# Four token mixers on one core: the order of all engines written out from an estimate, and weights split piece by piece

## The chip, the core and the metric

The kernel runs on one core of a Trainium2 chip. The metric is the device time of one execution in microseconds (us). A core has five instruction streams that run side by side and wait for each other through semaphores: PE (matrix products), DVE and ACT (element work on 128 partitions), POOL (a slower engine for element work) and SP (here it only issues DMAs). Each stream is executed in the order in which the program holds it, so a stream whose next instruction waits also holds up all that stands behind it.

## The reference, cut to what matters

Two layers, 256 tokens of width 1024, all in float32. The change concerns the middle step of each layer.

```python
x += 0.5 * rms(swiglu(rms(x)))             # FFN 1, inner width 2816
h = rms(x); p = h @ W_in                   # one projection, cut into column groups
y_nsa  = nsa_mixer(q, k..., v..., gates)   # 4 heads: compressed + selected + window
y_ret  = retention_mixer(q, k, v, g_in)    # 4 heads, chunks of 128
y_rwkv = rwkv7_mixer(p[rwkv columns])      # 4 heads, recurrence over chunks of 64
y_swa  = banded_attention(q, k, v, 128, sinks)
merged = sum(sigmoid(gate_m(h)) * (y_m @ P_m) for m in the four mixers)
x += rms(merged @ W_out)
x += 0.5 * rms(swiglu(rms(x)))             # FFN 2
```

Every weight matrix is read once per layer from HBM. Products with weights are made in three passes over numbers cut into a high and a low part (high x high, high x low, low x high), so each weight tile is first loaded raw, then copied to its high part by ACT (`whi`) and subtracted to its low part by DVE (`wlo`). This pair of instructions is called a split below.

## The kernel before, in words

The program runs FFN 1, the mixers, the product with W_out (`rows_out`) and FFN 2, twice. The change touches the mixers alone; instructions of the FFN stages and of `rows_out` are the same in both programs.

In the mixers there are two kinds of PE work. *Bulk* work has weights: projections into 512, 332 or 320 columns (`bulk_proj`, bank name `pj`), the four RWKV projections of 256 columns (`rwkv_proj`, `rwp`) and the branch products (`branch_block`, `z`). Each chunk `c` of the contraction takes three matmuls for each of the two token tiles `t` (`mm3`, L174 to L176). *Light* work has none: transposes (`tr`), attention scores (`sc`), the 32x32 solves of RWKV (`px`, `pq`), its recurrence (`pz`, `pu`, `psn`). Light work comes in chains: a few matmuls, then DVE, ACT or POOL instructions on their result, then the next matmuls.

`weave` writes the two kinds out in one list. Each light chain is a generator (a strand) that yields a number, the nanoseconds after which its next step may stand, or the name of a result that it needs. `weave` keeps one clock, `self.clk`, that only matmuls move, with a fixed cost for each. When a strand's time has come it is run, and otherwise the next piece of bulk work. Bulk pieces come in the order of the list `bulk`, the first whose inputs are done. After 2500 ns of light work in a row bulk is forced (`LIGHT`). What `weave` makes is only a priority: a list scheduler then places the instructions of each engine, with its own idea of when each could start, and splits of weights are lifted ahead by `high_priority(PRI)` in `stream`. Each bulk item calls `stream` for all its weights when it starts.

Memory: raw weights rotate through 4 buffers and split weights through 6 (`wraw`, `wsplit`), bulk results through 3 PSUM banks (`psA`), light results through 5 (`psB`), other mixer tiles through 29 buffers of 2 KB and 19 of 1 KB a partition (`NS2`, `NK1`).

Names used below. `pss` (L556) are the sums of squares of the RWKV keys: they need `sq` on DVE (L1061), and through POOL's `krs` and DVE's `rsb` they lead to `prs` and `kn` (L1084, L1087), then `bh` (L1092) and `ln`. `nsark` is the rotated key of the sparse attention, made by POOL (L545) and transposed by PE. `acc` (L1345) is the first use of a branch product `z`. `sm` (L602) is the softmax that is transposed next.

Of the kernel before, what the change touches and what calls it, by code (L numbers as in the profile page):

```python
# [21 lines left out]
NT = 2  # L22
# [78 lines left out]
NS2, NK1 = 29, 19  # L101
TAIL = 3
FL = 4
CY = 420
PRI, PRI2 = 60, 150
HOLD = 3
PROJ = (3, 1, 0, 2, 4, 5)
BRANCHES = (0, 1, 2)
WARM = 12
LIGHT, LIGHT_LOW = 2500.0, 425.0  # L110


class Trunk:
    def __init__(self, tc, A, out, layers=L, dbg=None):
        self.tc, self.nc, self.A, self.out = tc, tc.nc, A, out
        self.layers = layers
        self.dbg = dbg or {}
        self.uid = 0
        self.clk = self.light = 0.0
        self.pending = []  # L120
        self.feat = 0
# [46 lines left out]
    def mm3(self, out, a, b, first, last):  # L168

        mm = self.nc.tensor.matmul  # L170
        d = 3 * max(109.0, 2.5 + b[0].shape[-1] / 2.4)
        self.clk += d
        self.light = max(0.0, self.light - d)
# [14 lines left out]
    def psA(self, name="pa"):  # L188
        return self.ps.tile([P, 512], F32, tag="A", bufs=3, name=self.nm(name))

    def psB(self, name="pb"):
        return self.ps.tile([P, 512], F32, tag="B", bufs=5, name=self.nm(name))
# [39 lines left out]
    def pre_norm(self, t, xT, ss=None):  # L232
# [17 lines left out]
        def half(b):  # L250
# [6 lines left out]
            nc.vector.tensor_tensor(lo[:, 4 * b:4 * b + 4, t * P:(t + 1) * P], pv, dh.bitcast(F32), op=ALU.subtract)  # L257

# [188 lines left out]
    def bulk_proj(self, l, xT, c0, n, evac, key, lat=900, skew=False):  # L447

        w = [self.stream(self.A["w_in"][l][h * 512:(h + 1) * 512, c0:c0 + n], 4, n) for h in range(2)]
        pp = [self.psA("pj") for _ in range(NT)]  # L450
        order = [(c, t) for t in range(NT) for c in range(KC)] if skew else \
            [(c, t) for c in range(KC) for t in range(NT)]
        for c, t in order:
            if skew and t and c == 0:
                self.flush()
            ts_ = slice(t * P, (t + 1) * P)
            self.mm3(pp[t][:, 0:n], (xT[0][:, c, ts_], xT[1][:, c, ts_]), w[c // 4](c % 4, slice(0, n)),
                     c == 0, c == KC - 1)
            if t or skew:
                yield  # L460
        for t in range(NT):
            evac(t, pp[t])
        self.fin(key, lat)
# [4 lines left out]
    def fin(self, key, lat):  # L468
        self.done[key] = self.clk + lat

    def weave(self, strands, bulk):


        live = [[0.0, None, g] for g in strands]
        self.live = live
        cur, force = None, False
        while live or bulk or cur:
            ran = False

            if self.light > LIGHT:  # L480
                force = True
            elif self.light <= LIGHT_LOW:
                force = False
            if force and cur is None:
                cur = self.next_bulk(bulk)
            for s in [] if force and cur is not None else list(live):
# [4 lines left out]
                if s[0] > self.clk:  # L491
                    continue
                try:
                    r = next(s[2])
                    if isinstance(r, str):
                        s[1] = r
                    else:
                        s[0] = self.clk + r
                except StopIteration:
                    live.remove(s)  # L500
                ran = True
                break
            if ran:
                continue
            if cur is None:
                cur = self.next_bulk(bulk)
            if cur is not None:
                try:
                    next(cur)
                except StopIteration:  # L510
                    cur = None
                continue
            nxt = [s[0] for s in live if s[1] is None] + [self.done[s[1]] for s in live if s[1] in self.done]
            nxt += [self.when(b[0]) for b in bulk]
            nxt = [x for x in nxt if self.clk < x < 1e18]
            assert nxt, ([s[1] for s in live], [b[0] for b in bulk])
            self.clk = min(nxt)

    def next_bulk(self, bulk):
        for b in bulk:  # L520
            if self.when(b[0]) <= self.clk:
                bulk.remove(b)
                return b[1]

    def spawn(self, g):
        self.live.append([self.clk, None, g])
# [20 lines left out]
    def transposes(self, srcs):  # L547

        pt = self.psB("tr")
        for j, s in enumerate(srcs):  # L550
            self.nc.tensor.transpose(pt[:, j * P:(j + 1) * P], s, self.ident)  # L551
            self.tick(109)
        return pt

    def mm(self, out, a, b, cost, start=True, stop=True):
        self.nc.tensor.matmul(out, a, b, start=start, stop=stop)  # L556
        self.tick(cost)

    def mm4(self, out, a, b):

        for g in range(4):
            gs = slice(32 * g, 32 * g + 32)
            self.mm(out[gs], a[:, gs], b, 34)

    def tick(self, cost):
        self.clk += cost
        self.light += cost


    def attention(self, t, groups, score, pv, sink, mask_off, gate, evac):  # L570
# [6 lines left out]
        for e in range(groups):  # L577
# [10 lines left out]
            nc.vector.tensor_scalar(nm, mx, -SCALE, None, op0=ALU.mult)  # L588
            for i in range(2):
                nc.scalar.activation(sm[:, i, :], sm[:, i, :], AF.Exp, bias=nm[:, i:i + 1], scale=SCALE,  # L590
                                     accum_out=den[:, i:i + 1])
            if sink is not None:
                es = self.small(2, "es")
                nc.vector.tensor_add(es, nm, sink[1](e))
                nc.scalar.activation(es, es, AF.Exp)
                nc.vector.tensor_add(den, den, es)
# [8 lines left out]
        yield 6600  # L605
# [7 lines left out]
        yield 2400  # L613
        po = self.psB("po")
        for j in range(2):
            terms = list(zip(*[pv(j, hh, pts) for hh in range(2)]))
            for k, pair in enumerate(terms):
                for hh, (v, pT) in enumerate(pair):
                    self.mm(po[64 * hh:64 * hh + 64, j * P:(j + 1) * P], v, pT, 135, k == 0, k == len(terms) - 1)
# [13 lines left out]
    def swa(self, l, xT):  # L633
# [6 lines left out]
        def evac(t, ps):  # L640
            nc.scalar.activation(pv[t], ps[:, 0:512], AF.Copy)
            self.spawn(after(t))

        def after(t):
# [6 lines left out]
            yield 8820  # L651
# [3 lines left out]
            self.fin(f"swa_qk{t}", 749)  # L655
# [857 lines left out]
```

## Time and profile before

| | us |
|---|---|
| median of three runs (lowest, highest) | 1392.92 (1392.23, 1393.69) |
| profiled execution, its own time | 1393.8 |
| its span, first to last instruction | 1392.0 |
| mixers of the first layer, first bulk matmul to the first of W_out | 200.6 to 483.8 |
| mixers of the second layer | 887.5 to 1172.6 |

PE is busy for 1348.1 us of the span, 97%; DVE for 65%, ACT for 50%, POOL for 15%. The DMA engines are busy for about half to two thirds of the time. A matmul's busy time reaches into the next one's, since PE overlaps them; what a matmul costs in a row of equal ones is the step from start to start.

### The profile page before, as it was taken

The numbers are of one execution on the slowest core, as the hardware profiler recorded it, in microseconds if no ns is written. First come the engines' busy times: TensorE is split into PE (matmuls) and PEld (weight loads), VectorE is DVE, ScalarE is ACT, GpSimd is POOL, SyncE is SP. The second block draws the span as 40 slices with busy tenths as digits, with TensorE's granted clock in tenths as the row PEclk, the third lists the DMA queues.
The fourth block names the chain that finished last, engine by engine and source line by source line (L and its number), as shares of the span: only waits on it lengthen the run. The fifth ranks groups of instructions, "written<-read, shape, count | busy, mean of one in ns | idle before, by whom it ended". The sixth has DMA issues, their size and how long they took to land.

```text
span 1392.0 us, 24466 instructions
## 1 busy us (share of the span) xinstructions
PE 1348.1 (97%) x9756; PEld 1139.1 (82%) x9756; DVE 903.9 (65%) x1417; ACT 699.1 (50%) x1110; POOL 205.5 (15%) x269
## 2 busy tenths in 40 slices
PE   8999999898999999999999999998999999999998
PEld 7888878776778889888898888787777888888886
DVE  6666467748766666665566664687487656766643
ACT  6555456425344455564555554554353445555542
POOL 1000022603332110000000000335035220100000
PEclk9999999999999999999999999999999999999999
DMA  8865553435346646755647656434453556476662
GB/s 269 282 186 189 184 181 112 153 115 188 104 155 195 182 152 202 220 184 182 212 152 240 186 180 220 147 117 137 144 177 93 161 188 195 139 224 183 184 192 77
DMA packets 166146, 243.02 MB, mean 175 GB/s; under 512 B 9216, under 2 KB 120320, under 8 KB 165904
## 3 DMA queue, kind: packets, MB, share of 16 engines
q1 hardware_dynamic: 165248, 239.31, 54.3%
q8 instruction: 76, 1.25, 0.4%
q0 software_dynamic: 352, 1.10, 0.3%
q10 hardware_dynamic: 432, 1.05, 0.2%
q14 instruction: 38, 0.31, 0.1%
HBM read 240.38 MB, written 1.05 MB: 173 GB/s over the span
## 4 chain that ended last, share of the span: by engine, by line
PE 79%; DVE 8%; POOL 5%; ACT 3%; issue 2%; DMA 2%; POOLq 0%; DVEq 0%; SPq 0%; ACTq 0%
PE pf L209 20%; PE pf L210 10%; PE dn L174 6%; PE dn L176 6%; PE dn L175 6%; PE pj L174 6%; PE pj L176 5%; PE pj L175 5%; PE tr L551 1%; PE pg L175 1%; PE pg L174 1%; PE pg L176 1%; PE z L174 1%; DVE wlo L148 1%; PE z L176 1%
## 5 line engine op out<-in xcount | busy, mean ns | idle before, releaser
L148 DVE TENSOR_TENSOR wlo<-raw,whi 128x1024 fp32r<-128x1024 f32 (+1 forms) x420 | 516.7, 1237 | 295.1 <-ACT whi L147 292.2
L147 ACT ACTIVATE whi<-raw 128x1024 fp32r<-128x1024 f32 (+1 forms) x420 | 436.7, 1047 | 363.9 <-PE pj L176 90.4
L209 PE MATMUL pf<-xs,whi 128*128 128x512 f32 x1184 | 419.0, 399 | 0.0
L210 PE MATMUL pf<-xs,wlo 128*128 128x256 f32 x1184 | 332.5, 281 | 0.0
L209 PEld LDWEIGHTS pf<-xs,whi 128*128 128x128 f32 x1184 | 222.4, 188 | 54.9
L210 PEld LDWEIGHTS pf<-xs,wlo 128*128 128x128 f32 x1184 | 223.7, 189 | 0.0
L174 PE MATMUL pj<-whi,xs 128*128 128x512 f32 (+2 forms) x448 | 178.9, 399 | 1.0 <-DVE retg L912 1.0
L176 PE MATMUL pj<-whi,xs 128*128 128x512 f32 (+2 forms) x448 | 172.6, 385 | 0.0
L175 PE MATMUL pj<-wlo,xs 128*128 128x512 f32 (+2 forms) x448 | 172.0, 384 | 0.0
L174 PE MATMUL dn<-whi,hhi 128*128 128x512 f32 x352 | 137.3, 390 | 0.0
L175 PE MATMUL dn<-wlo,hhi 128*128 128x512 f32 x352 | 137.2, 390 | 0.0
L176 PE MATMUL dn<-whi,hlo 128*128 128x512 f32 x352 | 137.0, 389 | 0.0
L218 POOL TENSOR_SCALAR rstd<-ss 128x1 f32<-128x1 f32 x24 | 10.1, 422 | 800.7 <-ACT ja L274 773.2
L174 PEld LDWEIGHTS pj<-whi,xs 128*128 128x128 f32 x448 | 85.8, 192 | 23.5 <-issue 6.2
L176 PEld LDWEIGHTS pj<-whi,xs 128*128 128x128 f32 x448 | 85.8, 191 | 16.7 <-issue 0.5
L175 PEld LDWEIGHTS pj<-wlo,xs 128*128 128x128 f32 x448 | 85.9, 192 | 13.3
L176 PEld LDWEIGHTS dn<-whi,hlo 128*128 128x128 f32 x352 | 66.1, 188 | 13.8
L174 PEld LDWEIGHTS dn<-whi,hhi 128*128 128x128 f32 x352 | 66.1, 188 | 13.6
L175 PEld LDWEIGHTS dn<-wlo,hhi 128*128 128x128 f32 x352 | 66.1, 188 | 13.5
L174 PE MATMUL pg<-whi,xs 128*128 128x256 f32 x224 | 64.3, 287 | 0.0
L176 PE MATMUL pg<-whi,xs 128*128 128x256 f32 x224 | 63.5, 284 | 0.3 <-DVE xs L257 0.2
L175 PE MATMUL pg<-wlo,xs 128*128 128x256 f32 x224 | 63.5, 284 | 0.1
(346 smaller groups left out, 1821.6 us busy)
## 6 DMA issues: line engine op xcount, KB each, us to landing
raw<-in_w_in_dram SPq DMA_DIRECT2D x112, 512.0 KB, 3.5
raw<-in_ffn_w_gate_dram SPq DMA_DIRECT2D x88, 512.0 KB, 4.7
raw<-in_ffn_w_up_dram SPq DMA_DIRECT2D x88, 512.0 KB, 4.5
raw<-in_ffn_w_down_dram SPq DMA_DIRECT2D x88, 512.0 KB, 3.9
raw<-in_w_out_dram SPq DMA_DIRECT2D x16, 512.0 KB, 4.4
cw<-in_nsa_cmp_k_w_dram SPq DMA_DIRECT2D x8, 512.0 KB, 3.9
cw<-in_nsa_cmp_v_w_dram SPq DMA_DIRECT2D x8, 512.0 KB, 4.4
raw<-in_w_br_ret_dram SPq DMA_DIRECT2D x8, 512.0 KB, 4.0
```

Source lines behind the costliest of these rows:

```text
L147: nc.scalar.activation(hi, raw, AF.Copy)
L148: nc.vector.tensor_sub(lo, raw, hi.bitcast(F32))
L174: mm(out, a[0], b[0], start=first, stop=False)
L175: mm(out, a[0], b[1], start=False, stop=False)
L176: mm(out, a[1], b[0], start=False, stop=last)
L209: mm(ps, hi, x[:, c].rearrange("p a s -> p (a s)"), start=c == 0, stop=False)
L210: mm(ps[:, 0:S], lo, xh[:, c, :], start=False, stop=c == KC - 1)
L218: eng.tensor_scalar(r, ss[:, 0:1], k * EPS, None, op0=ALU.add)
L551: self.nc.tensor.transpose(pt[:, j * P:(j + 1) * P], s, self.ident)
```

## The change

The scheduler is switched off for all five engines in the mixers: what the program emits is the order. To emit it well, `Estimate` now follows each engine. Every instruction is noted when it is made: it starts when its engine's queue is free and its inputs are ready, and takes a time worked out from its size; PE's clock moves on by the matmul's cost and, where an input isn't ready or a PSUM bank isn't free, by the wait. A strand yields `self.at(tiles)`, the time at which the tiles are ready by the estimate, in place of a constant; `self.soon(tiles)` marks a step that needs no PE and is to be emitted up to 500 ns ahead of that time.

```diff
-NS2, NK1 = 29, 19
+NS2, NK1 = 33, 11
-PROJ = (3, 1, 0, 2, 4, 5)
+HALVES = [(4 * h + c, t) for h in range(2) for t in range(NT) for c in range(4)]
+ORDER = "first nsa rw3 rw1 rw0 rw2 g30 b30 g31 b31 g00 b00 g01 b01 qk v g g10 b10 g11 b11 g20 b20 g21 b21"
+RAWS, SPLITS, URGENT = 4, 6, 3
+BACKLOG, BUSY, MARGIN, APART, LEAD = 1500.0, 2500.0, 250.0, 1300.0, 500.0
...
+        if eng == "DVE":
...
+            d = 165.0 + n / 0.96
+        elif eng == "ACT":
+            d = 200.0 + 0.86 * n + (200.0 if extra else 0.0)
+        else:
+            d = 150.0 + 0.83 * n if op == "memset" else 200.0 + n * (2.6 if len(ins) > 1 else 1.8)
...
+        t = max(self.q[eng], self.when(*ins, out) + 80.0, self.clk - 3000.0)
+        self.q[eng] = t = t + d
...
+        w = max(self.when(*ins) + 80.0, self.hold.pop(self.key(out), 0.0))
+        if w > self.clk:
...
+            self.clk = w
+        self.clk += d
...
+            with tc.manual_schedule(engines=ALL):
+                self.weave([self.rwkv(l)], bulk)
```

`ORDER` names the bulk items: `first` (the projections of the sliding-window attention and of the first part of `nsa`, now in one item), the rest of `nsa`, the four RWKV projections, then gates `g` and branch products `b` of each mixer between the three retention items. Weights are no longer loaded by item: all pieces of the coming items stand in one list, and `feed` loads the next piece when a raw buffer is free and splits it when it has landed, up to six ahead; beyond three ahead only while DVE and ACT have less than 1500 ns of work before them.

```diff
+            raw, kh, n = q[self.split]
+            if not must and (est.when(raw) > est.clk or
+                             self.split - self.freed > URGENT and max(est.q["DVE"], est.q["ACT"]) > est.clk + BACKLOG):
+                return
...
+            small = not (force and cur is not None) and (visit or since >= APART or cur is None) and \
+                est.free_banks(1, est.clk) > 1
...
+                if est.q["DVE"] > est.clk + BUSY and cur is not None:
                     continue
+                if s[3] and s[0] < est.clk + LEAD or small and not s[3] and (not s[0] or s[0] + MARGIN <= est.clk):
+                    run = s
+                    break
```

So light work is visited at intervals of at least 1300 ns of bulk, and a step is taken when the estimate had its inputs ready 250 ns ago. Bulk work takes four chunks of one token tile, then four of the other, and the first tile is evacuated while the second is still being made; a branch product makes one token tile and then the other. In RWKV the chain from the keys to `kn` becomes a strand of its own (`removal`).

```diff
-        for c in range(nch):
-            yh = yT[c // 2]
-            for t in range(NT):
-                self.mm3(zs[t], ...
+        for t in range(NT):
+            z = self.psA("z")
+            for c in range(nch):
+                yh = yT[c // 2]
+                self.mm3(z, ...
...
-        nc.gpsimd.tensor_scalar(ag, ag, 0.5, 0.5, op0=ALU.mult, op1=ALU.add)
...
+        def removal():
+
+            yield "rw1"
...
+            self.fin("kn", kn)
+
+        self.spawn(removal())
```

Five POOL instructions of each layer go: a memset, the scaling of `ag`, two products of `t` and one of `bh`; DVE gets the last three and one more, on 128x2. All other instructions are the same in number and size on every engine. Lines of the new program are mostly L127, the helper that records each instruction.

Three places follow. First DVE, where `sq` is made in the first layer; `wlo` is the second half of a split, `den`, `rd`, `nm` and `es` belong to an attention, `xk` and `xr` are projected inputs of RWKV. Before:

```order
L585 TENSOR_REDUCE mx_2297<-sm_2299 128x2
L602 TENSOR_SCALAR sm_2278<-sm_2278,rd_2289 128x256 x2
L587 TENSOR_TENSOR mx_2297<-mx_2297,s_344_1885 128x2
L1060 TENSOR_SCALAR kr_2403<-xk_2071,vec 128x256
L588 TENSOR_SCALAR nm_2298<-mx_2297 128x2
L1060 TENSOR_SCALAR kr_2403<-xk_2071,vec 128x256
L594 TENSOR_TENSOR es_2306<-nm_2298,rowv_742 128x2
L148 TENSOR_TENSOR wlo_2641<-raw_2638,whi_2640 128x664
L1061 TENSOR_TENSOR sq_2404<-kr_2403 128x512
L596 TENSOR_TENSOR den_2296<-den_2296,es_2306 128x2
```

Now:

```order
L127 SCALAR_TENSOR_TENSOR xk_2410<-ppd_2495,vec,pp_2492 128x256
L127 TENSOR_TENSOR wlo_2525<-raw_2418,whi_2524 128x1024
L127 TENSOR_SCALAR kr_2570<-xk_2410,vec 128x256 x2
L127 TENSOR_TENSOR sq_2571<-kr_2570 128x512
L127 TENSOR_TENSOR wlo_2582<-raw_2420,whi_2581 128x1024
L127 TENSOR_TENSOR ppd_2588<-pp_2585 128x256
L127 SCALAR_TENSOR_TENSOR xr_2498<-ppd_2588,vec,pp_2585 128x256
```

`sq` moved from behind two attentions and a split to right behind the `xk` that it is made from, ahead of the work on the next projection `xr`.

Second PE, where it reads `sq`; `rwp` is the last RWKV projection, `tr`, `po` and `prs` are light work and `pj` bulk. Before:

```order
L175 MATMUL rwp_2363<-xs_191,whi_2359 128x256
L176 MATMUL rwp_2363<-xs_191,wlo_2360 128x256
L556 MATMUL pss_2420<-const,sq_2404 32x2 x16
L551 MATMUL tr_2452<-ident,sm_2278 128x128 x4
L551 MATMUL tr_2459<-ident,sm_2299 128x128 x4
L556 MATMUL po_2466<-pT_2391,swap_1881 64x128 x2
L556 MATMUL po_2466<-pT_2396,swap_1881 64x128 x2
L174 MATMUL pj_2537<-whi_2515,xs_191 128x320
```

Now:

```order
L127 MATMUL pj_2785<-wlo_2704,xs_191 128x512
L127 MATMUL pj_2785<-whi_2703,xs_191 128x512
L127 MATMUL pss_2792<-const,sq_2571 32x2 x16
L127 MATMUL tr_2812<-ident,sm_2383 128x128 x4
L127 MATMUL pj_2785<-whi_2715,xs_191 128x512
L127 MATMUL pj_2785<-wlo_2716,xs_191 128x512
```

`pss` stood right behind the last of the 192 matmuls of the four RWKV projections; it now stands 54 matmuls of 512 columns behind them. Of the light work that came with it (two groups of transposes and `po`) one group of transposes is left.

Third DVE, where the first branch products are taken from PSUM. Before:

```order
L1274 TENSOR_TENSOR sst_4375<-sst_4375,rsc_2219 128x128
L148 TENSOR_TENSOR wlo_4459<-raw_4456,whi_4458 128x1024
L1345 SCALAR_TENSOR_TENSOR acc_4402<-gate_4139,z_4388 128x512
L1345 SCALAR_TENSOR_TENSOR acc_4404<-gate_4141,z_4389 128x512
L148 TENSOR_TENSOR wlo_4602<-raw_4599,whi_4601 128x1024
```

Now:

```order
L127 SCALAR_TENSOR_TENSOR acc_3749<-gate_2757,z_3717 128x512
L127 SCALAR_TENSOR_TENSOR acc_3758<-gate_2783,z_3751 128x512
L127 TENSOR_TENSOR X_3784<-px_3767,const 128x128
L127 TENSOR_TENSOR X_3803<-px_3786,const 128x128
L127 SCALAR_TENSOR_TENSOR acc_3810<-gate_2920,z_3760 128x512
L127 TENSOR_TENSOR wlo_3817<-raw_3721,whi_3816 128x1024
```

The two `acc` no longer stand behind a split; On PE the two `z` of an item ended three matmuls apart before, and the next item's `z` came at once; now they end six matmuls apart.

In each layer's mixers PE's light work stands in 42 groups between bulk work before, and in 54 now.

## Rows read from the trace of the kernel before

**Rows 1.** Busy time by stretch: us, PE, PEld, DVE, ACT, POOL, granted clock, DMA, GB/s.

```profile
0.00:200.60 200.60, 194.83 (x1052) 167.62 (x1053) 127.39 (x156) 113.05 (x164) 7.89 (x20) 1.00 0.69 221
200.60:483.80 283.20, 270.60 (x2661) 221.10 (x2659) 191.38 (x392) 126.11 (x225) 88.70 (x100) 0.98 0.48 150
887.50:1172.60 285.10, 271.55 (x2661) 222.37 (x2659) 191.76 (x389) 126.24 (x225) 88.50 (x100) 0.98 0.47 149
```

**Rows 2.** Waits of PE, first layer's mixers: us in total, times, longest.

```profile
PE pss L556 <- DVE den L596: 2.6, 1, 2.6
PE po L556 <- issue: 2.5, 1, 2.5
PE tr L551 <- POOL nsark L545: 2.0, 1, 2.0
PE z L174 <- DVE acc L1345: 1.5, 1, 1.5
PE pj L174 <- DVE retg L912: 1.0, 1, 1.0
...
PE ln L556 <- DVE bh L1092: 0.4, 1, 0.4
```

**Rows 3.** Waits of PE, second layer's mixers.

```profile
PE tr L551 <- DVE sm L602: 2.6, 1, 2.6
...
PE ln L556 <- DVE bh L1092: 2.6, 1, 2.6
PE tr L551 <- POOL nsark L545: 1.9, 1, 1.9
...
PE prs L1084 <- DVE rsb L1071: 0.6, 1, 0.6
```

**Rows 4.** Busy time by stretch, where the granted clock falls; columns as in rows 1.

```profile
240.00:282.00 42.00, 36.87 (x356) 32.04 (x355) 30.85 (x59) 18.67 (x39) 25.03 (x32) 0.88 0.47 147
940.00:972.00 32.00, 27.34 (x257) 23.65 (x256) 22.93 (x38) 13.26 (x22) 18.20 (x25) 0.89 0.44 133
1022.00:1030.00 8.00, 5.35 (x52) 4.50 (x49) 8.00 (x18) 4.16 (x11) 3.97 (x5) 0.79 0.35 100
1073.00:1081.00 8.00, 6.47 (x27) 4.35 (x25) 6.56 (x11) 1.95 (x2) 5.55 (x5) 0.79 0.49 152
```

**Rows 5.** Timeline of all engines where PE waits for `sq`: start, us, instruction.

```profile
243.72 0.69 DVE L1061 TENSOR_TENSOR sq<-kr 128x512 f32<-128x512 f32 x1
...
244.55 0.44 PE L556 MATMUL pss<-const,sq 128*32 128x2 f32 x19 [2.55 <-DVE den L596]
```

**Rows 6.** Timeline where PE waits for a bank of `z`.

```profile
386.69 0.39 PE L176 MATMUL z<-whi,yl 128*128 128x512 f32 x1
387.88 1.27 DVE L1345 SCALAR_TENSOR_TENSOR acc<-gate,z 128x512 f32<-128x512 f32 x2
...
388.61 0.50 PE L174 MATMUL z<-whi,yh 128*128 128x512 f32 x1 [1.53 <-DVE acc L1345]
```

**Rows 7.** Timeline of PE around one group of light work.

```profile
356.28 0.39 PE L175 MATMUL pj<-wlo,xs 128*128 128x512 f32 x1
356.51 0.39 PE L176 MATMUL pj<-whi,xs 128*128 128x512 f32 x1
356.82 0.46 PE L556 MATMUL pz<-sst,ar 64*64 64x64 f32 x8
...
358.71 0.50 PE L174 MATMUL pj<-whi,xs 128*128 128x512 f32 x1
359.05 0.40 PE L175 MATMUL pj<-wlo,xs 128*128 128x512 f32 x1
```

**Rows 8.** Groups by line: count, busy us, mean ns of L602, first layer.

```profile
L602 DVE TENSOR_SCALAR sm<-sm,rd 128x256 f32<-128x256 f32 x12 | 4.9, 451 | 0.0
```

**Rows 9.** The same instruction in the second layer, timeline of all engines.

```profile
1024.28 2.17 DVE L602 TENSOR_SCALAR sm<-sm,rd 128x256 f32<-128x256 f32 x2
1024.29 1.26 POOL L545 TENSOR_TENSOR retr<-ra,rb 128x512 f32<-128x512 f32 x1
```

More of the change, by code (lines that the diff above doesn't have):

```diff
@@ L444, in c, with pieces @@
         return self.const[:, o:o + n]
[L447 to L459, printed above, removed]
+    def pieces(self, src, k, n):
+        sv = src.rearrange("(k p) n -> p k n", p=P)
+        kh = min(k, 1 << (1024 // n).bit_length() - 1)
+        return [(sv[:, h * kh:(h + 1) * kh, :], kh, n) for h in range(k // kh)]
@@ new lines, in soon, with fin @@
+    def soon(self, *aps):
+        return (self.at(*aps),)
+    def fin(self, key, *aps):
+        self.done[key] = self.at(*aps)
+    def weave(self, strands, bulk):
+        est = self.est
+        est.reset()
+        live = self.live = [[0.0, None, g, False] for g in strands]
+        self.fifo, self.loaded, self.split, self.taken, self.freed, self.lent = [], 0, 0, 0, 0, 0
+        ahead, cur, end, force, since, visit, start = [], None, 0.0, False, 1e9, False, True
+        while live or bulk or cur or ahead:
+            while bulk and (not ahead or len(self.fifo) - self.taken < SPLITS):
+                t = max(end, est.clk) + sum(b[3] for b in ahead)
+                b = next((b for b in bulk if self.when(b[0]) <= t), None)
+                if b is None:
+                    break
+                bulk.remove(b)
+                ahead.append(b)
+                self.fifo.extend(b[2])
+                if b[4]:
+                    self.done[b[4]] = t + b[3]
+            if start:
+                for _ in range(SPLITS - 1):
+                    self.feed(True)
+                est.reset()
+                start = False
+            self.feed()
+            if cur is None and ahead and self.when(ahead[0][0]) <= est.clk:
+                b = ahead.pop(0)
+                cur, end = b[1], est.clk + b[3]
+            if est.light > LIGHT:
@@ L511, in weave @@
                     cur = None
+                since += est.clk - t
                 continue
[L513 to L523, printed above, removed]
+            nxt = [s[0] + MARGIN for s in live if s[1] is None] + \
+                [self.done[s[1]] + MARGIN for s in live if s[1] in self.done]
+            nxt += [self.when(b[0]) for b in ahead + bulk]
+            nxt += [est.read.get(k, 0.0) for k in est.banks[1] if k]
+            nxt = [x for x in nxt if est.clk < x < 1e18]
+            assert nxt, ([s[:2] for s in live], [b[0] for b in bulk])
+            est.log.append((est.clk, min(nxt) - est.clk, "nothing to do", []))
+            est.clk = min(nxt)
     def spawn(self, g):
-        self.live.append([self.clk, None, g])
+        self.live.append([0.0, None, g, False])
     def rope(self, out_ap, src, t, nh, dup=False):
@@ L595, in attention @@
                 nc.scalar.activation(es, es, AF.Exp)
+            yield self.soon(sm, den)
+            if sink is not None:
                 nc.vector.tensor_add(den, den, es)
@@ L1199, in rwkv @@
[L1199 to L1209 removed]
+        yield self.at(rkk, vt, *mot)
@@ L1350, in branch_block, with later @@
         if last and b == 0:
-            self.spawn(self.later(2550, self.acc_split(b)))
+            self.spawn(self.later(b))
         elif last:
             self.pending = [lambda: list(self.acc_split(b))]
-    def later(self, lat, g):
-        yield lat
-        yield from g
+    def later(self, b):
+        yield self.at(*[self.acc[t][b] for t in range(NT)])
+        yield from self.acc_split(b)
     def late_dma(self, dst, src):
```

646 lines of the change are left out of this document (422 added, 224 removed).

## The prediction

> **What bounds the kernel now.** I read the busy times by stretch first. They show PE as the bound everywhere: in the first 200.6 us PE is busy for 194.83 at a clock of 1.00, and in the two mixers for 270.60 of 283.20 and 271.55 of 285.10 us [rows 1]. So the change can win only what PE loses in the mixers, and no other stage's instructions change. What is lost there is of two kinds. First idle time: 283.20 - 270.60 = 12.6 and 285.10 - 271.55 = 13.55, together 26.1 us. Second, the granted clock. It is at one of two levels, 2.4 or 1.2 GHz, and four stretches of the mixers hold all the time at the lower one; their mean shares are 0.88, 0.89, 0.79 and 0.79 [rows 4]. At half clock a stretch loses half of the time spent there, which is (1 - mean) times its length: 42 x 0.12 + 32 x 0.11 + 8 x 0.21 + 8 x 0.21 = 5.0 + 3.5 + 1.7 + 1.7 = 11.9 us. So 38.0 us of the profiled execution's 1393.8 can be won at most by a better order; the rest is PE's own work.
>
> I then read who ended the idle time, in both layers [rows 2, 3]. A few long waits make nearly all of it, on DVE or POOL results that light work needs: `pss` 2.6 and `z` on `acc` 1.5 (in the second layer again, rows of the same text), `nsark` 2.0 and 1.9, `ln` 0.4 and 2.6, `sm` up to 2.6, `po` 2.5. Weights don't appear among them: no row says that PE waited for a split. The timeline says what such a wait is. `sq` is made at 243.72, 0.69 us long, and PE starts `pss` on it at 244.55 after 2.55 us idle [rows 5]; the row names `den`, which came last by the semaphore, but the tile read is `sq`. In the order DVE had two attentions and a split ahead of `sq`, while PE had nothing but `pss` next. For `z` it is a PSUM bank: PE starts a bulk matmul at 386.69, then stands 1.53 us until DVE, which starts `acc` at 387.88, has emptied a bank [rows 6].
>
> The clock's falls lie at the same places: the stretches of [rows 4] are those around `pss` and `nsark`, `ln` and `nsark`, `sm`, and `z`. So a wait there costs itself and then some 1.7 us or more of slow matmuls.
>
> **The change part by part.** *The waits.* Where the new order shows more bulk work between producer and reader, I take the wait as gone. `sq` now stands right behind `xk` on DVE, and `pss` 54 matmuls of 512 columns later on PE; their step is 356.51 - 356.28 = 0.23 us [rows 7], so 54 x 0.23 = 12.4 us lie where 2.55 were missing. For `ln` I take the same from the same chain, since it starts at `pss`; so also `prs` (0.6). `z` ends six matmuls apart instead of three (1.4 us against 0.7), and `acc` has no split ahead of it; projections too leave their two banks at different times, which takes `retg`'s 1.0. Sum: `pss` 2.6 + 2.6, `ln` 0.4 + 2.6, `prs` 0.6, `z` 1.5 + 1.5, `retg` 1.0 = 12.8 us. The remaining 26.1 - 12.8 = 13.3 us (`nsark`, `po`, `sm` and small ones) I can't place by the order alone. The bounds are 13.3 won and, below nothing, as much again lost, if new waits of this kind come up. I take half, 6.7: the rule that places light work now counts queues of DVE, ACT and POOL, which the old constants did not, but POOL's part is the roughest. Waits won: 19.5.
>
> *The clock.* Of the 11.9 us, the falls at `pss`, `ln` and `z` go with their waits. The first stretch holds a longer fall at `pss` and a shorter at `nsark`: two thirds of 5.0 is 3.3; of the second's two falls one is at `ln`: 1.7; the fourth, at `z`, 1.7. That is 6.7. Of the other 5.2 I take half, as for their waits: 2.6. Clock won: 9.3, with bounds 0 and 11.9.
>
> *More groups of light work.* 54 in each layer in place of 42. What a change to light work and back costs is in [rows 7]: the light matmul starts 0.31 us after the last bulk one, where 0.23 is the step, and the first bulk matmul behind takes 359.05 - 358.71 = 0.34. That is 0.08 + 0.11 = 0.19 us a group, and 2 x 12 x 0.19 = 4.6 us lost. The bounds are 0, if the groups save changes among themselves, and 4.6.
>
> *DVE and POOL.* Three products go from POOL to DVE. DVE is busy for 191.38 of 283.20 us, POOL for 88.70 [rows 1]; neither is the bound, PE's work covers it, so I set it at nothing. If that cover is gone, at a place where PE waits for `bh`, DVE's side costs at most an instruction like `sq`, 0.69 us [rows 5], a layer.
>
> *Weights by pieces.* I set it at nothing, between 0 and nothing won: PE waits for no split now. A piece of 2 x 512 columns feeds 12 matmuls, 2.8 us at 0.23, so three pieces split ahead are 8 us of cover; no wait of [rows 2, 3] is half that. If the cover failed, PE would wait for a split, which then is late by one DVE instruction.
>
> *The seams.* Transposes of the next norm stand three matmuls earlier, 0.7 us, at the first seam, and six bulk matmuls later at the second one; I set the two against each other.
>
> Sum: 1393.8 - 19.5 - 9.3 + 4.6 = 1369.6 for the profiled execution. The median of the runs is 1392.92, 0.9 below it, so I forecast **1369 us** (rounded; 1.7% less). With all bounds at their good end it is 1393.8 - 38.0 = 1355.8, less 0.9: 1355. With the uncertain waits and half their falls staying, it is 1369 + 6.7 + 2.6 = 1378.
>
> **What speaks against it: DVE beside POOL.** `sm` on 128x256 takes 0.451 us on average [rows 8]. Where POOL's `retr` (1.26 us) starts beside it, two take 2.17, 1.27 more than twice the mean [rows 9]: just POOL's instruction. This wait of PE, 2.6 us in [rows 3], so comes about by POOL, and the new order doesn't know of it: the estimate prices a DVE instruction by its size alone (165 ns + elements / 0.96), each queue by itself. The Trainium skill says the same in "SBUF — State Buffer", section "Who interferes with whom": DVE and GpSimd share a pair of ports, which one of them holds for a whole instruction while the other fully blocks. By that rule, where the trace agrees with its 1.27 us, late DVE results would stay in the new order, and the sum would be that of the second rival below; by the order alone it is the forecast.
>
> **The rivals.** *All of it.* The estimate is good enough, and waits and falls go nearly wholly. For it: the waits are few and each has its cause in an order, not in a lack of room; DVE has 92 us free in a mixer. Against it: POOL. Time: 1355 to 1359, with up to 4.6 for the groups; 1357.
>
> *Slower: POOL's instructions make DVE late in a fixed order.* Place: the last DVE step before a light group. The estimate allows 0.25 us and 0.08 more; a delay of 1.27 leaves 0.94 us of wait. POOL is busy for 88.70 of 283.20 us, 31%, so 17 of the 54 groups of a layer could meet it, and with both layers 34 x 0.94 = 32 us. The old waits are gone (-26.1), the falls stay, since such waits leave PE as idle, and the groups cost 4.6: 1393.8 - 26.1 + 32 + 4.6 = 1404.3, less 0.9: 1403. It is slower than before from 24 such groups on, 12 a layer. For it: [rows 9]. Against it: most groups wait for ACT or for a DVE instruction that reads PSUM, and few rows of before name such a wait though POOL was as busy there.
>
> *The waits only move.* Light chains are as long as before, and with more and smaller groups PE meets the same results a little later. Then idle time, falls and time stay: 1393. For it: no instruction goes from PE. Against it: only 26.1 of 568 us are idle, so the chains as a whole have room.
>
> *The change doesn't do what it says*, for instance since a scheduler moves the instructions again: the built order shows that it doesn't, so I give it nothing.
>
> **How the numbers follow.** Forecast 0.54 (1369, its own range 1360 to 1380); all of it 0.21; waits move 0.10, of which 0.06 within 0.2% of before (2.8 us, about what a measurement of this kernel can tell from no change) and 0.02 on each side; slower by POOL 0.15. Faster by over 0.2%: 0.54 + 0.21 + 0.02 = 0.77; within it 0.06; slower 0.15 + 0.02 = 0.17. The range that should hold 8 in 10 goes from 1354, just under the good end of all bounds, to 1397, which takes in the waits that move and part of the slower case.
>
> **What would show it.** Right: `pss`, `ln` and `z` gone from PE's waits; PE's idle time in each mixer at 3 to 7 us; one or two falls of the clock in place of six; mixers of about 271 us. If the clock still falls in stretches without a wait, my link of falls to waits is wrong. If DVE rows of one kind take over twice their mean just before a wait of PE, POOL is the cause. If PE waits for `wlo`, the cover of three pieces was too small, which none of my cases holds. A PE whose busy time itself grows would mean that groups cost more than 0.19 us.

## The result and the profile after

The changed kernel takes 1369.35 us (median of four runs, 1366.55 to 1370.31); the kernel before, run beside it, 1393.31. The ratio is 0.9826, with a 95% interval of 0.9808 to 0.9844. The forecast was 1369. The profiled execution of the changed kernel took 1369.88 us with a span of 1368.1, 23.9 less than before's.

Nearly all of it lies in the mixers. Busy time by stretch, with columns as in [rows 1]:

```profile
0.00:200.60 200.60, 195.65 (x1053) 168.75 (x1053) 127.47 (x157) 112.41 (x164) 7.04 (x20) 0.99 0.68 217
200.60:475.60 275.00, 268.60 (x2662) 220.03 (x2661) 201.59 (x397) 127.56 (x228) 79.16 (x95) 0.99 0.50 156
...
879.30:1149.10 269.80, 265.50 (x2662) 217.56 (x2660) 201.09 (x394) 127.25 (x228) 79.17 (x95) 1.00 0.51 159
```

The first mixer stretch went from 283.20 to 275.00 us and the second from 285.10 to 269.80, together 23.5. PE's idle time in them went from 26.1 to 275.00 - 268.60 + 269.80 - 265.50 = 10.7 us. DVE is busy for 10 us more in each and POOL for 9 less; neither became the bound.

Waits of PE, first layer's mixers and then the second's (us in total, times, longest), against [rows 2, 3]:

```profile
PE px L127 <- issue: 2.6, 1, 2.6
PE sc L127 <- DVE swaqk L127: 1.4, 1, 1.4
PE pq L127 <- issue: 1.0, 1, 1.0
PE tr L127 <- DVE acc L127: 0.5, 1, 0.5
PE pj L127 <- DVE gate L127: 0.4, 1, 0.4
PE z L127 <- ACT gate L127: 0.4, 1, 0.4
```

```profile
PE pq L127 <- issue: 1.6, 2, 0.9
PE sc L127 <- DVE swaqk L127: 1.4, 1, 1.4
PE pj L127 <- DVE gate L127: 0.4, 1, 0.4
...
```

`pss`, `ln`, `prs`, `nsark`, `sm`, `retg` and the waits of `z` on `acc` are gone. What is left is new: PE stops inside runs of small matmuls with "issue" as the only reason, and it waits for `swaqk`, a copied transpose of the sliding-window attention. The clock falls twice in the mixers where it fell six times. These are the two stretches that hold it; both falls lie in the first layer, just behind its two longest waits:

```profile
226.00:234.00 8.00, 6.62 (x33) 5.90 (x32) 5.98 (x13) 4.74 (x14) 2.69 (x5) 0.79 0.43 133
325.00:333.00 8.00, 5.36 (x171) 4.05 (x163) 3.88 (x9) 1.94 (x5) 0.00 (x0) 0.79 0.26 83
```

By the rule used for [rows 4], half of the time at 1.2 GHz, they cost 8 x 0.21 = 1.7 us each, 3.4 in place of 11.9.

How the waits that went were replaced: `sq` is made on DVE at 253.9 us and PE reads it for `pss` at 275.2, 21 us later, where [rows 5] had 2.55 us of idle. The first two `acc`, which in [rows 6] held PE for 1.53 us, now start at 338.41 while PE goes on without a gap:

```profile
338.26 0.39 PE L127 MATMUL z<-whi,yh 128*128 128x512 f32 x1
...
338.41 1.28 DVE L127 SCALAR_TENSOR_TENSOR acc<-gate,z 128x512 f32<-128x512 f32 x2
...
338.49 0.39 PE L127 MATMUL z<-wlo,yh 128*128 128x512 f32 x1
```

The two waits that are left have different causes. The first, timeline of PE in the RWKV solve of the first layer (start, us, instruction, idle before):

```profile
324.24 0.39 PE L127 MATMUL pj<-whi,xs 128*128 128x512 f32 x1
324.56 0.54 PE L127 MATMUL px<-T,ln 32*32 32x32 f32 x39
327.74 0.40 PE L127 MATMUL px<-T,ln 32*32 32x32 f32 x25 [2.64 <-issue]
```

After 39 of 64 matmuls of one step PE stands for 2.64 us, though those behind the stop read the same tiles as those just ahead of it. The other is the chain ahead of `swaqk`, timeline of DVE, POOL, ACT and PE:

```profile
223.51 1.29 POOL L127 TENSOR_TENSOR nsarq<-ra,rb 128x512 f32<-128x512 f32 x1
...
223.92 0.89 DVE L127 TENSOR_TENSOR mx<-mx,s 128x2 f32<-128x2 f32 x1
...
224.75 0.73 POOL L127 TENSOR_TENSOR ra<-nsaa,const 128x256 f32<-128x256 f32 x1
...
224.85 0.67 DVE L127 TENSOR_SCALAR nm<-mx 128x2 f32<-128x2 f32 x1
...
225.43 1.21 DVE L127 TENSOR_TENSOR wlo<-raw,whi 128x1024 fp32r<-128x1024 f32 x1
...
226.56 0.41 DVE L127 TENSOR_TENSOR es<-nm,rowv 128x2 f32<-128x2 f32 x1
227.06 0.20 ACT L127 ACTIVATE es<-es 128x2 f32<-128x2 f32 x1 [0.57 <-DVE es L127]
227.17 0.37 ACT L127 ACTIVATE swaqk<-tr 128x256 f32<-128x256 f32 x1
...
227.92 1.13 PE L127 MATMUL sc<-swaqk,swaqk 64*128 64x256 f32 x4 [1.38 <-DVE swaqk L127]
```

`mx` and `nm` hold two numbers a partition, and yet take 0.89 and 0.67 us, where the medians of their kind in this trace are 0.16 and 0.17: each ends when the POOL instruction beside it ends or some 0.04 us later (223.51 + 1.29 = 224.80 for 223.92 + 0.89 = 224.81; 224.75 + 0.73 = 225.48 for 224.85 + 0.67 = 225.52), as `sm` did in [rows 9]. `es` and the exponentials on ACT stand behind them, and `swaqk` behind those. POOL is not the whole cause: on DVE the split `wlo` stands between `nm` and `es`, and ACT idles 0.57 us for `es` just ahead of `swaqk`.

### The profile page after: what moved, and what is told of

Same layout as the page of the kernel before. It is cut to its first block, busy times and chain, and to the rows that moved or that the text cites. A ratio compares the mean times of both kernels' runs of the same rounds, so it can differ in the third digit from the quotient of the medians.

```text
span 1368.1 us, 24477 instructions
## 1 busy us (share of the span) xinstructions
PE 1340.8 (98%) x9756; PEld 1133.9 (83%) x9756; DVE 921.7 (67%) x1425; ACT 695.2 (51%) x1110; POOL 185.8 (14%) x259
## 4 chain that ended last, share of the span: by engine, by line
PE 89%; DVE 3%; issue 2%; ACT 2%; POOL 1%; DMA 1%; DVEq 0%; POOLq 0%; ACTq 0%
PE pf L127 31%; PE pj L127 19%; PE dn L127 18%; PE pg L127 5%; PE rwp L127 3%; PE z L127 3%; PE tr L127 2%; ACT ja L127 1%; PE sc L127 1%; PE pq L127 1%; ACT whi L127 1%; PE pt L127 1%; POOL rstd L127 1%; PE po L127 1%; DVE wlo L127 1%
## 5 line engine op out<-in xcount | busy, mean ns | idle before, releaser
L127 DVE TENSOR_TENSOR wlo<-raw,whi 128x1024 fp32r<-128x1024 f32 (+2 forms) x420 | 517.2, 1241 | 270.7 <-ACT whi L127 268.7
L127 ACT ACTIVATE whi<-raw 128x1024 fp32r<-128x1024 f32 (+2 forms) x420 | 434.7, 1046 | 250.4 <-PE dn L127 56.1
L127 PE MATMUL pf<-xs,whi 128*128 128x512 f32 x1184 | 419.0, 399 | 0.0
L127 PE MATMUL pf<-xs,wlo 128*128 128x256 f32 x1184 | 332.5, 281 | 0.0
L127 PE MATMUL pj<-whi,xs 128*128 128x512 f32 (+2 forms) x896 | 294.6, 391 | 0.9 <-DVE gate L127 0.9
L127 PEld LDWEIGHTS pf<-xs,whi 128*128 128x128 f32 x1184 | 222.5, 188 | 55.0
L127 PEld LDWEIGHTS pf<-xs,wlo 128*128 128x128 f32 x1184 | 223.7, 189 | 0.0
L127 PEld LDWEIGHTS pj<-whi,xs 128*128 128x128 f32 x896 | 167.3, 189 | 34.6 <-issue 3.7
L127 PE MATMUL pj<-wlo,xs 128*128 128x512 f32 (+2 forms) x448 | 170.7, 381 | 0.0
L127 PE MATMUL dn<-whi,hhi 128*128 128x512 f32 x352 | 137.5, 391 | 0.0
L127 PE MATMUL dn<-wlo,hhi 128*128 128x512 f32 x352 | 137.1, 389 | 0.0
L127 PE MATMUL dn<-whi,hlo 128*128 128x512 f32 x352 | 137.0, 389 | 0.0
L127 POOL TENSOR_SCALAR rstd<-ss 128x1 f32<-128x1 f32 x24 | 10.1, 420 | 781.5 <-ACT ja L127 781.5
L127 PEld LDWEIGHTS pj<-wlo,xs 128*128 128x128 f32 x448 | 84.8, 189 | 12.6
L127 PE MATMUL pg<-whi,xs 128*128 128x256 f32 x448 | 85.3, 288 | 0.2 <-DVE xs L127 0.2
L127 PEld LDWEIGHTS dn<-whi,hlo 128*128 128x128 f32 x352 | 66.1, 188 | 13.8
L127 PEld LDWEIGHTS dn<-whi,hhi 128*128 128x128 f32 x352 | 66.1, 188 | 13.6
L127 PEld LDWEIGHTS dn<-wlo,hhi 128*128 128x128 f32 x352 | 66.1, 188 | 13.5
L127 PEld LDWEIGHTS pg<-whi,xs 128*128 128x128 f32 x448 | 71.9, 194 | 0.8 <-DVE xs L127 0.4
L127 PE MATMUL pg<-wlo,xs 128*128 128x256 f32 x224 | 64.1, 286 | 0.1
L127 ACT ACTIVATE hg<-pf 128x256 f32<-128x256 f32 x74 | 27.7, 374 | 58.2 <-PE pf L127 58.2
L127 DVE TENSOR_TENSOR hu<-hu,pf 128x256 f32<-128x256 f32 x74 | 30.9, 418 | 34.6 <-ACT hu L127 34.6
```

What stands on the lines that cost most here:

```text
L127: r = f(*a, **k)
```

## Experiments

All are timed against the kernel before in three rounds. Theory: the order by an estimate that knows the queues removes PE's waits, and with them the falls of the clock. The main rivals: it is enough that the order is fixed; it is the order inside the bulk items; POOL's hold on DVE decides.

**1. The scheduler on again.** The emission order is only a priority, as in the kernel before.

```diff
-            with tc.manual_schedule(engines=ALL):
-                self.weave([self.rwkv(l)], bulk)
+            self.weave([self.rwkv(l)], bulk)
```

> The changed program, but its emission order is only a priority again: the list scheduler places the instructions of each engine. On PE the order stays close (54 groups of light work per layer), on the other engines more moves. Theory (what wins is that the order of all engines is the one the estimate was made for): late DVE results behind splits and attentions come back, about half of the 15.4 us of idle time and of the 8.5 us of clock that were won is lost again: 1375 to 1386 us, with waits of PE of over 1 us on DVE results. Rival (what wins is what is emitted, and the scheduler keeps it nearly): within 3 us of the changed kernel's 1369.4.

Measured: 1372.66 us, ratio 0.9839 (0.9820 to 0.9858). The interval overlaps that of the changed kernel. The time is 3.3 us above it, below the theory's range and just outside the rival's 3 us. So the rival is nearer: that the order is fixed is worth some 3 us, which these runs can't tell from nothing. One wait of 2.3 us in each layer is new (`pz` on `sst`), and the `swaqk` wait is nearly gone.

**2. The estimate without queues.** An instruction of DVE, ACT or POOL starts in the estimate as soon as its inputs are ready.

```diff
-        t = max(self.q[eng], self.when(*ins, out) + 80.0, self.clk - 3000.0)
+        t = max(self.when(*ins, out) + 80.0, self.clk - 3000.0)
```

> The changed program with an estimate that leaves out the engines' queues: an instruction of DVE, ACT or POOL starts as soon as its inputs are ready. Theory (light steps come late enough only because the estimate knows what stands ahead on their engine): steps are placed too early where DVE or ACT has work before them; PE's idle time in the two mixers goes from 10.7 us back to 20 or more, clock falls from two to five or more, the time to 1380 to 1395 us. Rival (fixed order, spacing of 1300 ns and the bank rules do it, queues hardly matter): idle time 10 to 14 us, 1367 to 1373 us.

Measured: 1469.69 us, ratio 1.0537 (1.0513 to 1.0560): 100 us slower than the changed kernel, far beyond the theory's range. PE's idle time is 320.80 - 280.06 = 40.7 us in the first mixers and 43.5 in the second, and the clock's mean there is 0.95. The longest waits of the first layer:

```profile
PE pss L127 <- DVE sq L127: 6.6, 1, 6.6
PE tr L127 <- DVE sm L127: 6.1, 4, 3.3
PE lw L127 <- ACT tw L127: 5.9, 1, 5.9
...
```

The kernel before, with constants and a scheduler, had 2.6 for `pss`. So the change lives by the queues in the estimate. The edit does two things that this run doesn't tell apart: results look ready too early, and the two rules that hold work back while DVE or ACT is full (`BACKLOG`, `BUSY`) read queues that no longer add up.

**3. The old order inside the items.** Projections and branch products make their two token tiles chunk by chunk in turn, and evacuate both at the end.

```diff
-HALVES = [(4 * h + c, t) for h in range(2) for t in range(NT) for c in range(4)]
+HALVES = [(c, t) for c in range(KC) for t in range(NT)]
...
-            if c == KC - 1:
-                o[t] = evac(t, pp[t])
             yield
+        for t in range(NT):
+            o[t] = evac(t, pp[t])
```

(and the same in `branch_block`)

> The changed program, but projections and branch products make their two token tiles in turn chunk by chunk, as before, so that both are evacuated at the end, three matmuls apart. Theory (z and retg waits went since a bank is emptied while the other tile is made): these waits come back, 1.5 and 1.5 for z and 1.0 for a projection, with a clock fall of 1.7 us or more for some: 1373 to 1379 us. Rival (the waits went because no split stands ahead of the evacuation any more; the order inside an item does nothing): 1368 to 1371 us.

Measured: 1395.75 us, ratio 1.0019 (1.0005 to 1.0033). The direction is the theory's, but the size is 26 us where I had 4 to 10: more than the whole gain. Waits of PE, first layer:

```profile
PE pj L127 <- DVE acc L127: 2.4, 1, 2.4
PE z L127 <- DVE acc L127: 2.4, 1, 2.4
PE z L127 <- DVE gate L127: 2.3, 1, 2.3
PE pq L127 <- issue: 2.3, 1, 2.3
PE pj L127 <- ACT gate L127: 2.2, 3, 1.0
...
```

The timeline at the second of them:

```profile
320.04 1.06 ACT L127 ACTIVATE whi<-raw 128x1024 fp32r<-128x1024 f32 x1 [6.85 <-issue]
...
320.26 0.39 PE L127 MATMUL z<-whi,yl 128*128 128x512 f32 x1
...
321.14 1.23 DVE L127 TENSOR_TENSOR wlo<-raw,whi 128x1024 fp32r<-128x1024 f32 x1 [1.50 <-ACT whi L127]
322.28 1.28 DVE L127 SCALAR_TENSOR_TENSOR acc<-gate,z 128x512 f32<-128x512 f32 x2
...
323.01 0.78 PE L127 MATMUL z<-whi,yh 128*128 128x512 f32 x1 [2.36 <-DVE acc L127]
```

A split is emitted when the last matmul on a weight piece gives its buffer back, and that is the item's last step: so `whi` and `wlo` stand ahead of `acc`, DVE idles for 1.50 us until `whi` is done, and PE waits for the bank behind both. The trace has a split right ahead of the evacuation at every long wait for a bank in this layer but that on `retg` (1.4 us), where other light work of DVE stands there.

**4. The order of before, fixed on PE.** The kernel before, its emission order fixed on PE, the other engines scheduled.

```diff
-            self.weave([self.rwkv(l)], bulk)
+            with tc.manual_schedule(engines={mybir.EngineType.PE}):
+                self.weave([self.rwkv(l)], bulk)
```

> The kernel before with the order on PE fixed to what it emits with its old constants; the scheduler still places the other engines. Theory (a fixed order is worth nothing without the estimate): the constants know nothing of queues, so PE meets late results more often: 1395 to 1430 us, slower than before. Rival (the scheduler was what harmed, and the emitted order is good by itself): 1370 to 1385 us.

Measured: 1402.81 us, ratio 1.0057 (1.0032 to 1.0082), as the theory had it, near the low end of its range: the old waits, the longest of them grown. First layer:

```profile
PE pss L556 <- DVE den L596: 4.0, 1, 4.0
PE pj L174 <- DVE retg L912: 3.2, 1, 3.2
...
```

**5. Steps of the solve spread out.** A `px` or `pq` step may stand only 4.2 us, by the estimate, behind the burst before it.

```diff
-            yield self.at(*X)
+            last = self.est.clk
+            yield max(self.at(*X), last + 4200.0)
```

(and the same ahead of `px`)

> The changed program, but in the RWKV solve a burst of 32x32 matmuls (64 of px, 128 of pq) may stand only 4.2 us by the estimate behind the burst before it. In the changed kernel px and pq bursts start 2.7 to 4.5 us apart and PE stands inside four of them for 2.6, 1.0, 0.9 and 0.6 us with nothing to wait for but its own instructions; in the kernel before they were 3.2 to 5.4 us apart and none stood. Theory (PE runs through instructions faster than they are fetched): these 5.2 us go, and with them the clock fall at 328.8 us, 1.7 us: 1361 to 1365 us. Rival (the stop belongs to a place in the code and not to the spacing): the same stops stay, or come up in other bursts, and the time stays within 3 us of 1369.4.

Measured: 1362.75 us, ratio 0.9785 (0.9770 to 0.9800), wholly below the changed kernel's interval. No wait on "issue" in a mixer is left, and no fall of the clock in either mixer. Windows of both mixers, and of 8 us around the wait for `swaqk`:

```profile
201.20:469.00 267.80, 264.72 (x2662) 217.56 (x2661) 203.42 (x397) 127.43 (x229) 81.43 (x95) 1.00 0.52 160
872.40:1140.50 268.10, 264.96 (x2662) 217.69 (x2660) 203.20 (x394) 127.53 (x228) 81.48 (x95) 1.00 0.52 160
...
226.00:234.00 8.00, 6.63 (x47) 5.59 (x46) 7.10 (x15) 5.28 (x14) 3.26 (x6) 1.00 0.44 122
```

So the stops depend on how closely the bursts follow each other: in this trace the spaced bursts start 6.0 to 8.7 us apart, in the changed kernel 2.7 to 8.3 and mostly under 4.6. The place in the program counts too, which is half of the rival. These are the changed kernel's windows from its first stop to its second and from its third to its fourth, with PE's matmuls and weight loads counted:

```profile
326.00:343.00 17.00, 15.13 (x384) 11.25 (x384) 10.35 (x23) 5.30 (x10) 0.53 (x1) 0.90 0.45 147
1000.30:1006.30 6.00, 5.29 (x128) 3.97 (x128) 4.46 (x14) 2.54 (x6) 0.00 (x0) 1.00 0.63 210
```

That is 768 and 256 instructions, multiples of 256. The profile's page of the same execution has 9756 matmuls and as many weight loads, and these transfers of the instruction queues:

```profile
PE 1340.8 (98%) x9756; PEld 1133.9 (83%) x9756; DVE 921.7 (67%) x1425; ACT 695.2 (51%) x1110; POOL 185.8 (14%) x259
...
q8 instruction: 76, 1.25, 0.3%
```

One transfer of `q8` comes for every 19512 / 76 = 257 of PE's instructions. The ten traces that hold such stops (those of runs 5 and 7 don't) have 30 of 0.5 us or more in the mixers. In each trace, with PE's semaphore instructions counted in, they lie a multiple of 256 instructions apart, to within one, and at each PE goes on 1.1 to 1.5 us after the end of a transfer of `q8`. By all this PE waits there for the next 256 of its own instructions. What sets the time of these transfers is not shown.

The last window of run 5 has the same wait for `swaqk` as the changed kernel, 1.36 us, but the clock stays at 1.00 where it was 0.79. Up to the fall the two executions are alike: at the same instructions PE was busy for 6.42 of 7.80 us in the changed kernel (222.00 to 229.80) and for 6.43 in run 5 (222.56 to 230.36).

**6. POOL's hold in the estimate.**

```diff
...
+        if eng == "POOL":
+            self.span.append((t, t + d))
+        elif eng == "DVE" and op in ("tensor_tensor", "tensor_add", "tensor_sub", "tensor_scalar", "tensor_copy") and \
+                not any(self.key(x) in self.psum for x in ins):
+            for s, e in self.span[-40:]:
+                if s <= t < e:
+                    t = min(e, t + 900.0)
...
+        self.psum.add(self.key(t))
```

> The changed program with an estimate in which a DVE instruction that reads no PSUM (tensor_tensor and tensor_scalar forms) and would start beside a running POOL instruction waits for that one's end, at most 0.9 us. Theory (PE's wait for swaqk, 1.4 us in each layer, comes from DVE held up by POOL): light steps behind such results stand later, the two waits go and with the first of them the clock fall at 229.8 us, 1.7 us: 1363 to 1367 us. Rival (later steps meet other work; what goes at one place comes up at others): 1367 to 1373 us with waits of PE at other results.

Measured: 1363.34 us, ratio 0.9790 (0.9776 to 0.9805). Time and clock came out as the theory had it: the waits for `swaqk` and, in the profiled execution, all falls in the mixers are gone. But the rival is partly right too: other waits are there, first layer:

```profile
PE pz L127 <- DVE sst L127: 1.5, 1, 1.5
PE tr L127 <- DVE acc L127: 1.0, 1, 1.0
PE px L127 <- issue: 0.5, 1, 0.5
```

The edit also moved the bursts of the solve, so its gain is not that of `swaqk` alone.

**7. Both.** The edits of 5 and 6 together.

> The changed program with both edits: bursts of the solve 4.2 us apart and POOL's hold on DVE in the estimate. Theory: the two gains add up, 5.2 + 1.7 + 2.8 + 1.7 = 11.4 us: 1358 us (1356 to 1363), PE's idle time in each mixer 2 to 3 us, no fall of the clock in the mixers. Rival: not additive, 1363 to 1370 us.

Measured: 1362.84 us, ratio 0.9791 (0.9774 to 0.9807), the same as with either: the gains don't add up. PE's idle time is 2.8 us in each mixer, as expected, but that is hardly below run 5's 3.1: waits of 1.4 (`tr` on POOL's `retr`) and 1.1 us (`tr` on `acc`) took the place of the one for `swaqk`. What is left of the mixers is PE's own work, 265 of 268 us.

**8. The arithmetic back on POOL.** The scaling of `ag` and the three products are on POOL again.

```diff
+        nc.gpsimd.tensor_scalar(ag, ag, 0.5, 0.5, op0=ALU.mult, op1=ALU.add)
...
-        nc.vector.scalar_tensor_tensor(bh, ag, 1.0, e2, op0=ALU.add, op1=ALU.mult)
+        nc.gpsimd.tensor_tensor(bh, ag, e2, op=ALU.mult)
...
```

> The changed program with the three products of t and bh and the scaling of ag back on POOL as before (POOL busy for about 88 instead of 79 us in a mixer, DVE for 5 us less). Theory (few light steps stand behind a DVE instruction that POOL can hold up): no or one more wait of about 1 us in each layer, 1368 to 1374 us. Rival (my slower case: DVE beside POOL decides in a fixed order): 4 or more new waits of PE of about 1 us in each layer on DVE results, 1378 us or more.

Measured: 1367.18 us, ratio 0.9820 (0.9803 to 0.9837), with POOL busy for 85.9 us a mixer in place of 79.2. The theory holds, with a time just below its range: with 7 us more of POOL one wait on DVE grows, `tr` on `acc` from 0.5 and 0.4 us to 1.0 in each layer, and the time can't be told from the changed kernel's.

**9. The old pairs, evacuation ahead of the split.** As 3, but an item's last weight piece is given back only behind its evacuations, and the item no longer pauses (`yield`) ahead of them. Against run 3:

```diff
-            if t:
+            if t and c < KC - 1:
                 done(c)
-            yield
+            if (c, t) != HALVES[-1]:
+                yield
         for t in range(NT):
             o[t] = evac(t, pp[t])
+        done(KC - 1)
```

(and the same in `branch_block`)

> As the run with the old pairs (two token tiles in turn, 1395.75 us), but an item's last weight piece is given back only behind the evacuation of both tiles, so the split that it sets free is emitted behind that evacuation and not ahead of it on ACT and DVE. Theory (the 26 us of the old pairs come from a split of 1.06 us on ACT and 1.23 us on DVE right ahead of an evacuation that must be done 1.4 us later): most bank waits on acc, gate and retg go, PE's idle time from 17 us in a mixer to 8 to 11: 1374 to 1382 us. Rival (the slack of six matmuls, 1.4 us, is too short in itself with three banks): 1388 us or more.

Measured: 1372.37 us, ratio 0.9859 (0.9839 to 0.9879). 23 of the 26 us of run 3 are back, more than the theory asked. So the old pair order with 1.4 us of slack is nearly as good as the new one; what it can't bear is other work ahead of the evacuation. The edit keeps off both a split and the light work that could step in at the pause; that it was mostly the split is read from run 3's trace, not from this run alone. Of the bank waits 1.0 (`retv`), 0.5 (`gate`) and 0.4 us (`retg`) are left.

**10. One split piece ahead.**

```diff
-RAWS, SPLITS, URGENT = 4, 6, 3
-BACKLOG, BUSY, MARGIN, APART, LEAD = 1500.0, 2500.0, 250.0, 1300.0, 500.0
+RAWS, SPLITS, URGENT = 4, 6, 1
+BACKLOG, BUSY, MARGIN, APART, LEAD = -1e9, 2500.0, 250.0, 1300.0, 500.0
```

> The changed program, but after the start a weight piece is split only when no split piece is left unread but the one in use, so one piece ahead instead of three to six. My prediction set the split by pieces at nothing because three pieces are 8 us of cover; one piece is 12 matmuls, 2.8 us, against 1.06 us on ACT, 1.23 us on DVE and what is queued there. Theory (the cover of three is what hides it): PE waits for wlo at many pieces, 1 us each at 20 to 60 of the 150 pieces of both layers: 1390 to 1430 us. Rival (the order of the queues hides it with one piece as well): 1367 to 1375 us, no wait for wlo or whi above 0.5 us.

Measured: 1432.22 us, ratio 1.0283 (1.0260 to 1.0306), just above the theory's range. Waits of PE, first layer:

```profile
PE pj L127 <- DVE wlo L127: 9.3, 13, 1.5
PE pj L127 <- ACT whi L127: 4.5, 4, 1.9
...
PE rwp L127 <- DVE wlo L127: 2.5, 3, 1.1
```

In the kernel before and in the changed one PE waits for no split; so the cover of three pieces is used, and the time it hides is some 60 us, in waits and in the falls of the clock that come with them (mean 0.97 in both mixers).

Not tried alone: the order of the items (`ORDER`), the strand `removal` and the buffer counts.

## Why the prediction came out right, and where its steps were wrong

The total is right because two errors cancel, which is luck: the waits gave 4.1 us less than predicted, and the added groups cost 4.15 us less. By the sum's own terms, in the profiled executions:

| term | predicted | measured |
|---|---|---|
| waits of PE won | 19.5 | 26.1 - 10.7 = 15.4 |
| clock won | 9.3 | 11.9 - 3.4 = 8.5 |
| cost of more groups | 4.6 | 0.45 |
| DVE, POOL, pieces, seams | 0 | 0.4 won outside the mixers (span less mixers, 823.7 to 823.3) |

*The waits I named.* All eight went, 12.8 us, as worked out from the order. For `pss` and its chain the reason stands: 21 us lie between producer and reader.

*The waits I couldn't place.* Of the 13.3 us I had half won. All of the old ones went too (`nsark`, `sm`, `po`), but 10.7 us are there in the end, so only 2.6 were won net. This is the step that failed, "half of the uncertain waits": the new ones are 5.2 us inside bursts of small matmuls and 2.8 us for `swaqk`. The order of before had one such stop as well, 2.5 us at `po` [rows 2], right behind a `pq` step. In the new order the first three `px` steps of a layer start 6.3 to 8.0 us apart, before 7.4 to 10.1; run 5 took the stops away and brought 6.6 us. No term of the prediction was about the time in which PE gets its instructions.

*The clock.* 8.5 of 9.3. The link of falls to waits held in one direction: in both kernels' mixers each of the eight falls stands within 4 us behind the beginning of a wait of 1.4 us or more. It does not hold in the other: the wait for `swaqk` comes in both layers of the changed kernel and brings a fall in one, and in run 5 it brings none. The trace of before had said so too: three of its nine waits of 1.5 us or more, `po` and `z` in the first layer and `pss` in the second, bring no fall. So "a wait costs itself and then some 1.7 us" is not a price that each wait pays. The clock also differs between executions of one program: its mean was 0.986 to 0.995 in 30 executions of the kernel before, which took 1387.9 to 1397.0 us, and 0.993 to 0.996 in the four of the changed one. By the rule of [rows 4] the means over all of them, 0.9903 and 0.9950, give some 6.7 us for the clock in the whole program (an estimate: 1392.0 x 0.0097 - 1368.1 x 0.0050), where the mixers of the two profiled executions give 8.5.

*More groups.* Here the term was mis-sized. At full clock PE's busy time in the mixers is 270.60 + 271.55 - 11.9 = 530.25 us before and 268.60 + 265.50 - 3.4 = 530.7 after: 12 more groups in each layer cost some 0.45 us in all and not 4.6, and with this the terms give 15.4 + 8.5 - 0.45 = 23.45 of the 23.5 us. The 0.19 us of [rows 7] was read at one group of 64x64 matmuls and charged to all; by the sum the added groups don't pay it. Run 5, with two groups more in each layer and no fall in the mixers, has 264.72 + 264.96 = 529.7.

*DVE and POOL.* Nothing that run 8 could measure. *Weights by pieces.* Nothing, and for the reason given: with a cover of one piece (run 10) the waits for splits that I had named come. What I did not see is the other side of this part. A split is now emitted at the end of an item, on the two engines that must empty its banks. With the old order inside the items that alone would have eaten the gain (run 3), and runs 3 and 9 together show that it is the work ahead of the evacuation, mostly the split, and not the bank's 1.4 us. My text gave the two reasons for `z`, six matmuls in place of three and no split ahead of `acc`, as one; by run 9 the second carries nearly all.

*The rivals.* POOL's hold on DVE is real: `mx` and `nm` took 0.89 and 0.67 us, to the end of POOL's instruction. The Trainium skill says in "SBUF — State Buffer", section "Who interferes with whom", that one of the two holds the shared ports for its whole instruction while the other blocks; at these two instructions the trace agrees. But the hold had a part in one wait of 1.4 us in a layer and did not make 17 of 0.94. My count took each group beside POOL as a loss; how much slack the other results have was not measured. "All of it" (1357 us) was not reached, and runs 5 to 7 show what stands between: 1362.75 us is the best version here, 0.9785 of before. "The waits only move" is what happened to some 8 of the 26 us.

## What to carry to other kernels

When an order is written from an estimate, the engines' queues are the part that counts: without them the same program was 100 us slower, while handing the list back to a scheduler cost 3 us, too few to be told from none. A filler job that is emitted "when its buffer comes free" stands ahead of whatever is emitted next on those engines; release the buffer behind the evacuation, not ahead of it. Uncertain waits should be entered as waits that move, not as waits half gone, and the cost of a visit should be read from PE's busy time at full clock, not from one place.

## What the runs showed of the hardware

PE can outrun its own instruction stream. In and just behind steps of 64 or 128 matmuls of 32x32 it stood for up to 3.0 us with no engine to wait for, at places that lie multiples of 256 instructions apart, and went on 1.1 to 1.5 us after the end of a transfer of the instruction queue; with the steps 6.0 to 8.7 us apart it stood in none. A DVE instruction on two numbers a partition took 0.89 us beside POOL, where the median is 0.16. And the granted clock did not answer in the same way to the same wait: after the same instructions, with PE busy for 6.42 and 6.43 of 7.80 us, it fell to half in one execution and stayed at 1.00 in another.
